# Where the 128-column scores stand among TensorE's attention products in a decoder layer

## The chip, the cores and the metric

The kernel runs on one core of a Trainium2 chip. The metric is the device time of one execution in microseconds (us). TensorE multiplies matrices, VectorE (DVE), ScalarE (ACT) and GpSimd (POOL) do the elementwise work, and SyncE (SP) issues most of the transfers.

## The reference

One layer over 1024 tokens of width 1024, in float32. The input is normalised and modulated, and one projection makes all that follows: a gated convolution branch of 31 taps, 24 attention heads of 64 columns in three groups of 8, and gates.

```python
# (window, dilation) of a group; a query attends keys t, t-d, ..., t-window
DILATION_GROUPS = ((128, 1), (512, 4), (2048, 16))
scores = jnp.einsum('bdhnqe,bdhnke->bdhnqk', qb, kb) * (e ** -0.5)
scores = jnp.where(mask, scores, NEG_INF)
m = jnp.max(scores, axis=-1)
p = jnp.exp(scores - m[..., None])
o = jnp.einsum('bdhnqk,bdhnke->bdhnqe', p, vb) / p.sum(-1)[..., None]
...
merged = sigmoid(g_conv) * y_conv + sigmoid(g_att) * y_att
x = rmsnorm(x + gate * (merged @ w_o)) * final_g
```

Within a group the sequence is cut into subsequences by the dilation, and a block of 128 queries sees its own block of keys and, where there is one, the block before it. The first group has a previous block for 7 of its 8 blocks of queries, the second for every other block, the third for none.

## The kernel before

**Precision.** A product of two float32 matrices is made of three products of parts: each operand is split into a high part and a low part, and high x high, high x low and low x high are added up in PSUM (`mm3`, lines 73 to 75, for the projections). For a score the parts of keys lie one under the other on the 128 partitions (64 rows high, 64 low), with the queries' high part twice, so that two products do: the keys with `q` (line 880), and with `ql`, the low part of the queries over zeros (line 881).

**Stages.** The start makes the normalised input; then follow the projections of the convolution branch, while DVE works through the taps; then the attention with the projections of keys, queries and one gate beside it; then the merge, the last product and the norm. TensorE, DVE, ACT and SP run in the order in which the code is written in the attention (a manual schedule).

**The attention** is a loop over slots (lines 1093 to 1140). A slot issues half of a half unit of projection (4 of 8 steps of 128 rows, 12 products of 512 columns, by `next(stream)`), and then the attention's own products of three stages that are in flight:

- `values` of the slot 4 earlier (line 916): the stationary operand is a block of values, 64 columns, the moving one the weights of the softmax in two parts, `ph` and `pl`. A product moves 256 columns of queries or 128. The code calls the first block's three products of 256 `wide`, the others `narrow`. The third group has only products of 128, all `narrow`.
- `turn` of the slot 2 earlier (line 895): transposes of 128 x 128 of the exponentials `sb`, 2 to 4 in a slot, with the unit matrix `ident`. ACT and DVE then split the transposed result into `ph` and `pl` (lines 713 and 716).
- `scores` of the slot itself (lines 880 and 881): the stationary operand is a block of queries, 128 columns; the moving one is a block of keys, 128 columns, or two blocks, 256. A slot takes two blocks of queries of one head, so it has four score products: two of 128 and two of 256, four of 256, or in the third group four of 128. DVE then adds the mask and finds the row's extreme (line 884), ACT takes the exponential (line 888).

A head pair `n` takes 8 slots, four for each head; `st_` counts them. The tile `s` of PSUM for scores has two buffers, and so has `sb`. Keys and queries reach the tiles `k2`, `q2` and `ql` of a head by SP's copies (line 812) from the parts that a projection left, slots ahead of the head's first score.

**The order within a slot** is written out by hand. Lines 1118 and 1119 lay the values and transposes in one row: transpose, wide value, transpose, the narrow values, wide value, transpose, wide value, transpose. That row is issued; then the scores are issued behind it, block by block of queries, high part and low part; then comes the next slot's projection.

Of the kernel before, what the change touches and what calls it, by code (L numbers as in the profile page):

```python
# [16 lines left out]
P = 128  # L17
# [22 lines left out]
def layer(ctx: ExitStack, tc: tile.TileContext, a, out):  # L40
    nc = tc.nc
# [131 lines left out]
    with sbuf_pool("start") as st, tc.manual_schedule(  # L173
# [168 lines left out]
        for kt in range(KT):  # L342
# [9 lines left out]
            c = slice(kt * P, (kt + 1) * P)  # L352
# [273 lines left out]
    for d in range(KT):  # L626
        w, sg_ = ahead
# [186 lines left out]
    def move_kq(n, part, h):  # L814
        i = turn_of(n, h)
        if not part:
            k2[n, h], q2[n, h] = head_tile(f"k{i}", "k2"), head_tile(f"q{i}", "q2")
        move(k2[n, h], 0, n, part, 0, 0, h)
        move(k2[n, h], 64, n, part, 0, 1, h)
        move(q2[n, h], 0, n, part, 1, 0, h)  # L820
        move(q2[n, h], 64, n, part, 1, 0, h)
        move(q_low[i], 0, n, part, 1, 1, h)
# [28 lines left out]
    class Attend:  # L851
# [19 lines left out]
        def scores(self, st_):  # L871
            tp, h, spans, o = self.spans(st_)
            stats = self.stats
            k, q, ql = k2[self.n, h], q2[self.n, h], self.ql[h]
            ps = psa.tile([P, 512], F32, name="s", tag="s")
            sb = self.sb[st_] = ap_.tile([P, 512], F32, name="sb", tag="sb", bufs=2)
            for t, c, w in spans:
                k0 = t * P + P - w
                ts_, ks = slice(t * P, (t + 1) * P), slice(k0, k0 + w)
                nc.tensor.matmul(ps[:, c:c + w], q[:, ts_], k[:, ks], start=True, stop=False)  # L880
                nc.tensor.matmul(ps[:, c:c + w], ql[:, ts_], k[:, ks], start=False, stop=True)  # L881
            for t, c, w in spans:
                mk = mask2 if self.g == 2 else mask[:, 256 - w:256]
                nc.vector.tensor_tensor_reduce(  # L884
                    out=sb[:, c:c + w], in0=ps[:, c:c + w], in1=mk, scale=-SCALE, scalar=3e38, op0=add, op1=ALU.min,
                    accum_out=stats[:, t, h, 1:2])
            for t, c, w in spans:
                nc.scalar.activation(sb[:, c:c + w], sb[:, c:c + w], AF.Exp, bias=stats[:, t, h, 1:2],  # L888
                                     scale=-1.0, accum_out=stats[:, t, h, 0:1])
# [182 lines left out]
    beside, heads, ahead_ao = {}, {}, []  # L1072

    def in_steps(it, slots):
        for x in slots:
            beside.setdefault(x, []).append(it)

    def moves(n, part, h):
        move_kq(n, part, h)
        yield  # L1080
# [11 lines left out]
    with tc.manual_schedule(engines={nc.tensor.engine, nc.vector.engine, nc.scalar.engine, nc.sync.engine}):  # L1092
        for slot_ in range(-LEAD, 4 * units - LEAD):
            due, lows[:] = lows[:], []
            for low in due:
                low()
            after, prepared = next(stream)

            wide, narrow, turns, rest = [], [], [], []
            if VAL <= slot_ < stages + VAL:  # L1100
                n, st_ = divmod(slot_ - VAL, 8)
                rest.append(heads[n].values(st_))
                wide, narrow = next(rest[0])
                if st_ == 7:
                    del heads[n]
            if TURN <= slot_ < stages + TURN:
                n, st_ = divmod(slot_ - TURN, 8)
                rest.append(heads[n].turn(st_))
                turns = [next(rest[-1]) for _ in range(0, heads[n].spans(st_)[3], P)]
            row = turns[:1] + wide[:1] + turns[1:2] * bool(wide) + narrow + wide[1:2]  # L1110
            row += turns[1 + bool(wide):3] + wide[2:] + turns[3:]
            assert len(row) == len(turns) + len(wide) + len(narrow)
            for product in row:
                product()
            for x in rest:
                assert next(x, None) is None
            if 0 <= slot_ < stages:
                n, st_ = divmod(slot_, 8)
                if st_ == 0:
                    heads[n] = Attend(n)  # L1120
                heads[n].scores(st_)
            for n, part in made:
                move_kq(n, part, 0)
                in_steps(moves(n, part, 1), [slot_ if n == 0 else slot_ + 1 if part else 8 * n - 4])
            made[:] = []
            if after:
                after()
            for c in beside.pop(slot_, ()):
                next(c)
            if prepared and prepared[1] < units:  # L1130
                prepared[0](prepared[1])
            if 0 <= slot_ < stages and st_ == 7:
                heads[n].store_stats()
                if order[n][1] == 2:
                    in_steps(combine(order[n][0]), [slot_ + 1 + x for x in STEPS])
        assert not beside and next(stream, None) is None
        for low in lows:
            low()
# [152 lines left out]
```

## Time and profile before

| | us |
|---|---|
| median of 3 runs | 1257.31 |
| lowest and highest | 1256.59 and 1257.95 |
| the profiled execution | 1258.8 |
| its span in the trace | 1257.0 |
| first score to last value, from the span's start | 672 to 1070 |

The profile is one execution recorded on the chip. Times are counted from the span's start. PE is TensorE's matmuls, PEld its loads of weights (the stationary operand), which overlap the matmuls; PEclk is the clock that TensorE was granted, in tenths of full speed. In a row of the timeline stand the start, the duration, the engine, the line of the code, the operation, the tiles (written<-read), then the stationary operand's shape (128*64 is 128 partitions by 64 columns) and the moving one's (128x256). In a row of groups, xN is the number of instructions, and behind the bar stand the busy time in us and the mean duration in ns. Matmuls are pipelined: their records overlap and their ends are modelled, so the distance between starts tells more than a duration.

### The profile page before, as it was taken

The page shows a single profiled execution, that of the slowest core. Times are in us where ns is not written, and L with a number is a line of the kernel's source. Part 1 is how long each engine was busy: PE and PEld are TensorE (multiplying, and loading weights), DVE is VectorE, ACT ScalarE, POOL GpSimd, SP SyncE. Part 2 cuts the span into 40 slices and gives each one's busy share as a digit, 9 for nine tenths or more (in the row PEclk, how much of TensorE's full clock was granted, in tenths as well). Part 3 has the DMA queues.
Part 4 walks back from the last instruction along what each step waited for, and adds up shares of the span by engine and source line. Part 5 has one row for each costly group of instructions (what it writes and reads, how often), then busy time and mean ns, then how long its engine had stood idle before and what let it go on. Part 6 is the DMA issues. An engine that isn't in the chain of part 4 may idle for free.

```text
span 1257.0 us, 16947 instructions
## 1 busy us (share of the span) xinstructions
PE 1233.3 (98%) x6208; PEld 1033.5 (82%) x6208; DVE 909.0 (72%) x1496; ACT 511.7 (41%) x1023; POOL 91.5 (7%) x79
## 2 busy tenths in 40 slices
PE   5999999999999999999999999999999999999997
PEld 4877888888888888888888888888888888887886
DVE  6776999999999986873325657777776762448554
ACT  4554202111222135931015656666666665345211
POOL 0000000000000000000031111111111012100000
PEclk9999999999999999999999999999999999999999
DMA  9531311311211112455636555665575563668231
GB/s 362 174 122 59 118 51 59 109 59 51 74 61 51 51 53 82 127 174 193 191 85 150 133 131 145 164 172 144 158 186 146 133 185 120 205 224 294 100 101 67
DMA packets 89751, 165.35 MB, mean 132 GB/s; under 512 B 28547, under 2 KB 42179, under 8 KB 89669
## 3 DMA queue, kind: packets, MB, share of 16 engines
q1 hardware_dynamic: 72992, 157.67, 42.0%
q10 hardware_dynamic: 16676, 6.61, 1.9%
q8 instruction: 49, 0.80, 0.3%
q14 instruction: 34, 0.27, 0.1%
HBM read 105.74 MB, written 27.04 MB: 106 GB/s over the span
## 4 chain that ended last, share of the span: by engine, by line
PE 94%; DMA 2%; DVE 1%; ACT 1%; issue 0%; SPq 0%; ACTq 0%; DVEq 0%
PE d L73 22%; PE d L75 22%; PE d L74 22%; PE o L916 4%; PE t L895 2%; PE d L1195 2%; PE d L1194 2%; PE d L469 2%; PE d L1196 2%; PE d L467 2%; PE d L468 2%; PE s L881 2%; PE s L880 2%; PE d L251 1%; PE d L249 1%; PE d L250 1%
## 5 line engine op out<-in xcount | busy, mean ns | idle before, releaser
L73 PE MATMUL d<-hh,whi 128*128 128x512 f32 x1072 | 421.4, 393 | 0.0
L74 PE MATMUL d<-hl,whi 128*128 128x512 f32 x1072 | 418.4, 390 | 1.9 <-DVE hl L349 1.9
L75 PE MATMUL d<-hh,wlo 128*128 128x512 f32 x1072 | 418.7, 391 | 0.0
L408 DVE SCALAR_TENSOR_TENSOR v<-u,cw,v 128x1024 f32<-128x1024 f32 x232 | 280.6, 1285 | 0.0
L75 PEld LDWEIGHTS d<-hh,wlo 128*128 128x128 f32 x1072 | 201.4, 188 | 42.6
L74 PEld LDWEIGHTS d<-hl,whi 128*128 128x128 f32 x1072 | 201.6, 188 | 41.4 <-DVE hl L349 2.8
L73 PEld LDWEIGHTS d<-hh,whi 128*128 128x128 f32 x1072 | 201.6, 188 | 38.9 <-issue 0.2
L57 ACT ACTIVATE whi<-wraw 128x512 fp32r<-128x512 f32 (+1 forms) x106 | 85.8, 830 | 212.7 <-PE d L74 204.8
L58 POOL TENSOR_TENSOR wlo<-wraw,whi 128x512 fp32r<-128x512 f32 (+1 forms) x56 | 82.1, 1481 | 644.0 <-ACT whi L57 643.9
L884 DVE CUSTOM_DVE_ANT_0 sb<-s,mask 128x128 f32<-128x128 f32 (+1 forms) x192 | 59.9, 350 | 68.3 <-PE s L881 67.7
L888 ACT ACTIVATE sb<-sb,stats 128x128 f32<-128x128 f32 (+1 forms) x192 | 84.9, 444 | 39.0 <-DVE stats L884 38.7
L916 PE MATMUL o<-ph,vt 128*64 128x128 f32 (+1 forms) x432 | 70.9, 270 | 0.0
L895 PE MATMUL t<-ident,sb 128*128 128x128 f32 x280 | 70.8, 274 | 0.0
L58 DVE TENSOR_TENSOR wlo<-wraw,whi 128x1024 fp32r<-128x1024 f32 (+1 forms) x50 | 57.4, 1149 | 14.7 <-ACT whi L57 14.1
L713 ACT ACTIVATE ph<-t 128x384 fp32r<-128x384 f32 (+2 forms) x96 | 45.7, 476 | 37.8 <-PE t L895 31.5
L916 PEld LDWEIGHTS o<-ph,vt 128*64 128x64 f32 x432 | 50.0, 135 | 8.8
L716 DVE TENSOR_TENSOR pl<-t,ph 128x384 fp32r<-128x384 f32 (+2 forms) x96 | 52.0, 542 | 4.2 <-ACT ph L713 3.7
L916 PE MATMUL o<-pl,vt 128*64 128x128 f32 (+1 forms) x216 | 52.9, 261 | 0.0
L1194 PE MATMUL d<-oh,hh 128*128 128x512 f32 (+1 forms) x136 | 51.3, 377 | 0.0
L1196 PE MATMUL d<-oh,hl 128*128 128x512 f32 (+1 forms) x136 | 51.3, 377 | 0.0
L880 PE MATMUL s<-k,q 128*128 128x128 f32 (+1 forms) x192 | 51.1, 291 | 0.0
L634 DVE TENSOR_TENSOR gs<-d,sgc 128x512 f32<-128x512 f32 x16 | 11.1, 692 | 54.9 <-PE d L75 48.9
(227 smaller groups left out, 1909.6 us busy)
## 6 DMA issues: line engine op xcount, KB each, us to landing
wraw<-in_w_t SPq DMA_DIRECT2D x67, 512.0 KB, 3.9
k<-kqp SPq DMA_DIRECT2D x96, 128.0 KB, 2.4
q<-kqp SPq DMA_DIRECT2D x96, 128.0 KB, 2.5
wa<-in_w_ada SPq DMA_DIRECT2D x16, 512.0 KB, 6.6
ql<-kqp SPq DMA_DIRECT2D x48, 128.0 KB, 2.4
wg<-wscr SPq DMA_DIRECT2D x48, 128.0 KB, 3.1
wraw<-in_w_v SPq DMA_DIRECT2D x11, 512.0 KB, 3.6
x<-in_xT SPq DMA_DIRECT2D x8, 512.0 KB, 10.2
```

The source lines that it names most:

```text
L57: nc.scalar.activation(hi, raw, AF.Copy)
L58: (lo_eng or nc.vector).tensor_sub(lo, raw, hi.bitcast(F32))
L73: nc.tensor.matmul(ps, lh, rh, start=start, stop=False)
L74: nc.tensor.matmul(ps, lh, rl, start=False, stop=False)
L75: nc.tensor.matmul(ps, ll, rh, start=False, stop=stop)
L408: nc.vector.scalar_tensor_tensor(d, u[:, k:k + S], cw[:, ct, k:k + 1], d, op0=mult, op1=add)
L880: nc.tensor.matmul(ps[:, c:c + w], q[:, ts_], k[:, ks], start=True, stop=False)
L888: nc.scalar.activation(sb[:, c:c + w], sb[:, c:c + w], AF.Exp, bias=stats[:, t, h, 1:2], scale=-1.0, accum_out=stats[:, t, h, 0:1])
L895: yield from ((lambda c=c: nc.tensor.transpose(ps[:, c:c + P], sb[:, c:c + P], ident)) for c in range(0, o, P))
L916: nc.tensor.matmul(out_, l, r, **kw))
L1194: nc.tensor.matmul(ps, hh[:, k, c], rh, start=k == 0, stop=False)
L1196: nc.tensor.matmul(ps, hl[:, k, c], rh, start=False, stop=k == KT - 1)
```

## The change

`scores` no longer issues its products itself. It hands them out as a list, with the width of each (128 or 256), and goes on to DVE's and ACT's part when it is called again. The loop over slots then builds the row of values and transposes as before, and marks each entry twice: whether it is light (a value, whose stationary operand has 64 columns) and whether it is long (a transpose or a value of 256 columns). Ahead of a light entry, where what stands before it is long (or nothing stands before it), it puts the next of the slot's short scores, those of 128 columns. Short scores that find no place are issued behind the row, and the scores of 256 columns behind those.

```diff
             for t, c, w in spans:
                 k0 = t * P + P - w
                 ts_, ks = slice(t * P, (t + 1) * P), slice(k0, k0 + w)
-                nc.tensor.matmul(ps[:, c:c + w], q[:, ts_], k[:, ks], start=True, stop=False)
-                nc.tensor.matmul(ps[:, c:c + w], ql[:, ts_], k[:, ks], start=False, stop=True)
+                for i, x in enumerate((q, ql)):
+                    products.append((w, lambda c=c, w=w, l=x[:, ts_], r=k[:, ks], i=i: nc.tensor.matmul(
+                        ps[:, c:c + w], l, r, start=i == 0, stop=i == 1)))
+            yield products
...
-            row = turns[:1] + wide[:1] + turns[1:2] * bool(wide) + narrow + wide[1:2]
-            row += turns[1 + bool(wide):3] + wide[2:] + turns[3:]
-            for product in row:
-                product()
...
+            short = [p for w, p in score if w == P]
+            row = []
+            for x, light, long_ in ([(x, False, True) for x in turns[:1]] + [(x, True, True) for x in wide[:1]] +
+                                    [(x, False, True) for x in turns[1:2] * bool(wide)] +
+                                    [(x, True, False) for x in narrow] + [(x, True, True) for x in wide[1:2]] +
+                                    [(x, False, True) for x in turns[1 + bool(wide):3]] +
+                                    [(x, True, True) for x in wide[2:]] + [(x, False, True) for x in turns[3:]]):
+                if short and light and (not row or row[-1][1]):
+                    row.append((short.pop(0), False))
+                row.append((x, long_))
+            for product, _ in row:
+                product()
+            for product in short + [p for w, p in score if w > P]:
+                product()
```

The order on the other engines stays: DVE, ACT, POOL and SP issue the same instructions in the same order. On TensorE the scores' line is 882 now, the transposes' 898 and the values' 919.

First, TensorE's queue in a slot of the second group, behind the projection's 12 products, before the change. `t<-ident,sb` is a transpose, `o<-ph,vt` and `o<-pl,vt` are values, `s<-k,q` and `s<-k,ql` scores; the numbers in 64x256 are the columns of weights and of the moving operand for values, and 128 partitions and moving columns for scores and transposes.

```order
L895 MATMUL t<-ident,sb 128x128
L916 MATMUL o<-ph,vt 64x256
L895 MATMUL t<-ident,sb 128x128
L916 MATMUL o<-ph,vt 64x128 x2
L916 MATMUL o<-pl,vt 64x128
L916 MATMUL o<-ph,vt 64x256
L895 MATMUL t<-ident,sb 128x128
L916 MATMUL o<-pl,vt 64x256
L880 MATMUL s<-k_4719,q_4720 128x128
L881 MATMUL s<-k_4719,ql 128x128
L880 MATMUL s<-k_4719,q_4720 128x256
L881 MATMUL s<-k_4719,ql 128x256
```

The same slot in TensorE's queue after the change:

```order
L898 MATMUL t<-ident,sb 128x128
L882 MATMUL s<-k_4719,q_4720 128x128
L919 MATMUL o<-ph,vt 64x256
L898 MATMUL t<-ident,sb 128x128
L882 MATMUL s<-k_4719,ql 128x128
L919 MATMUL o<-ph,vt 64x128 x2
L919 MATMUL o<-pl,vt 64x128
L919 MATMUL o<-ph,vt 64x256
L898 MATMUL t<-ident,sb 128x128
L919 MATMUL o<-pl,vt 64x256
L882 MATMUL s<-k_4719,q_4720 128x256
L882 MATMUL s<-k_4719,ql 128x256
```

The two short scores moved from the row's end to places behind the first and the second transpose, each ahead of a value; the two long scores now follow the last value.

Second, TensorE's queue in a slot whose values are of the third group and whose scores are as well, before the change:

```order
L895 MATMUL t<-ident,sb 128x128
L916 MATMUL o<-ph,vt 64x128 x2
L916 MATMUL o<-pl,vt 64x128
L916 MATMUL o<-ph,vt 64x128 x2
L916 MATMUL o<-pl,vt 64x128
L895 MATMUL t<-ident,sb 128x128
L880 MATMUL s<-k_5122,q_5123 128x128
L881 MATMUL s<-k_5122,ql 128x128
L880 MATMUL s<-k_5122,q_5123 128x128
L881 MATMUL s<-k_5122,ql 128x128
```

And after it:

```order
L898 MATMUL t<-ident,sb 128x128
L882 MATMUL s<-k_5122,q_5123 128x128
L919 MATMUL o<-ph,vt 64x128 x2
L919 MATMUL o<-pl,vt 64x128
L919 MATMUL o<-ph,vt 64x128 x2
L919 MATMUL o<-pl,vt 64x128
L898 MATMUL t<-ident,sb 128x128
L882 MATMUL s<-k_5122,ql 128x128
L882 MATMUL s<-k_5122,q_5123 128x128
L882 MATMUL s<-k_5122,ql 128x128
```

Here one short score of four moved, behind the first transpose; the other three stay behind the row.

More of the change, by code (lines that the diff above doesn't have):

```diff
@@ L874, in scores @@
             k, q, ql = k2[self.n, h], q2[self.n, h], self.ql[h]
+            products = []
             ps = psa.tile([P, 512], F32, name="s", tag="s")
@@ L1109, in layer @@
                 turns = [next(rest[-1]) for _ in range(0, heads[n].spans(st_)[3], P)]
-            row = turns[:1] + wide[:1] + turns[1:2] * bool(wide) + narrow + wide[1:2]
-            row += turns[1 + bool(wide):3] + wide[2:] + turns[3:]
-            assert len(row) == len(turns) + len(wide) + len(narrow)
-            for product in row:
-                product()
-            for x in rest:
-                assert next(x, None) is None
+            score = []
             if 0 <= slot_ < stages:
@@ L1120, in layer @@
                     heads[n] = Attend(n)
-                heads[n].scores(st_)
+                rest.append(heads[n].scores(st_))
+                score = next(rest[-1])
+            short = [p for w, p in score if w == P]
[8 more added lines that the diff above has]
+                row.append((x, long_))
+            assert len(row) - len([p for w, p in score if w == P]) + len(short) == len(turns) + len(wide) + len(narrow)
+            for product, _ in row:
+                product()
+            for product in short + [p for w, p in score if w > P]:
+                product()
+            for x in rest:
+                assert next(x, None) is None
             for n, part in made:
```

## The prediction

> **What bounds the kernel now.** I read the page first, for the busiest engine and its clock.
>
> ```profile
> span 1257.0 us, 16947 instructions
> PE 1233.3 (98%) x6208; PEld 1033.5 (82%) x6208; DVE 909.0 (72%) x1496; ACT 511.7 (41%) x1023; POOL 91.5 (7%) x79
> PEclk9999999999999999999999999999999999999999
> ```
>
> TensorE is busy for 98% of the span at full granted clock, so only its own steps can be shortened. Next the table of stretches for the attention, 672 to 1071 us (columns: stretch, its length, then busy time and instructions of PE, PEld, DVE, ACT and POOL, the clock, the share of the DMA engines), and the table of TensorE's waits over the whole program.
>
> ```profile
> 672.00:1071.00 399.00, 399.00 (x2507) 345.25 (x2507) 267.11 (x755) 246.50 (x679) 63.52 (x45) 1.00 0.58 151
> PE d L249 <- ACT wh L237: 12.5, 1, 12.5
> PE d L74 <- DVE hl L349: 1.9, 2, 1.1
> PE d L75 <- DVE wlo L58: 1.2, 1, 1.2
> PE d L251 <- DVE hl L230: 0.4, 1, 0.4
> ```
>
> In the attention TensorE never waits for anybody (none of the four waits is of an attention line), DVE works 267 of 399 us and ACT 247. What sets the time of this stage is how quickly one product follows the other. A matmul's own duration does not tell that, since products overlap in the records. The starts of the weight loads do: a load starts when the product before its own starts. So the time from the load of X to the next load is the step from the product before X to X. Here are the loads of one slot (start, duration; L895 transposes, L916 values, L880 and L881 scores, L73 to L75 the projection).
>
> ```profile
> 719.44 0.19 PEld L75 LDWEIGHTS d<-hh,wlo 128*128 128x128 f32 x1
> 719.67 0.14 PEld L895 LDWEIGHTS t<-ident,sb 128*128 128x128 f32 x1
> 719.90 0.13 PEld L916 LDWEIGHTS o<-ph,vt 128*64 128x64 f32 x1
> 720.01 0.14 PEld L895 LDWEIGHTS t<-ident,sb 128*128 128x128 f32 x1
> ...
> 720.29 0.14 PEld L916 LDWEIGHTS o<-pl,vt 128*64 128x64 f32 x1
> 720.35 0.14 PEld L916 LDWEIGHTS o<-ph,vt 128*64 128x64 f32 x1
> 720.43 0.14 PEld L895 LDWEIGHTS t<-ident,sb 128*128 128x128 f32 x1
> 720.53 0.14 PEld L916 LDWEIGHTS o<-pl,vt 128*64 128x64 f32 x1
> 720.64 0.19 PEld L880 LDWEIGHTS s<-k,q 128*128 128x128 f32 x1
> 720.76 0.19 PEld L881 LDWEIGHTS s<-k,ql 128*128 128x128 f32 x1
> 720.87 0.19 PEld L880 LDWEIGHTS s<-k,q 128*128 128x128 f32 x1
> 720.98 0.19 PEld L881 LDWEIGHTS s<-k,ql 128*128 128x128 f32 x1
> 721.10 0.19 PEld L73 LDWEIGHTS d<-hh,whi 128*128 128x128 f32 x1
> ```
>
> Each step is the longer of two things: the stream of the product before, and the load of this one. Behind a projection product of 512 columns it takes 0.23 (719.44 to 719.67), all stream. A value after a transpose takes 0.11 (719.90 to 720.01): the transpose is a long product. A value of 64 weight columns after a value of 128 columns takes 0.06 (720.29 to 720.35). A score, 128 weight columns, takes 0.11 after a score of 128 columns (720.76 to 720.87). Is that its load, or the stream of the score before it? The matmul records answer: there, the next record starts when the stream before it is over.
>
> ```profile
> 720.76 0.22 PE L880 MATMUL s<-k,q 128*128 128x128 f32 x1
> 720.82 0.27 PE L881 MATMUL s<-k,ql 128*128 128x128 f32 x1
> 720.93 0.33 PE L880 MATMUL s<-k,q 128*128 128x256 f32 x1
> ```
>
> The first short score really starts at 720.76 (the next load's start), and the second's record begins 0.06 later; the second really starts at 720.87 (the load of the third), and the third's record begins at 720.93, again 0.06 later. So a short score streams for 0.06 and the array then stands 0.05 until 128 columns of weights are in. Short scores in a row, and the long product behind them, pay 0.11 each for a stream of 0.06. That is the waste the change can touch.
>
> **The change, part by part.** Another slot, with four short scores in a row; the load at 753.16 is the fourth behind the one at 752.72.
>
> ```profile
> 752.29 0.13 PEld L916 LDWEIGHTS o<-pl,vt 128*64 128x64 f32 x1
> 752.35 0.20 PEld L916 LDWEIGHTS o<-ph,vt 128*64 128x64 f32 x2
> 752.47 0.13 PEld L916 LDWEIGHTS o<-pl,vt 128*64 128x64 f32 x1
> ...
> 752.72 0.19 PEld L881 LDWEIGHTS s<-k,ql 128*128 128x128 f32 x1
> ...
> 753.16 0.19 PEld L74 LDWEIGHTS d<-hl,whi 128*128 128x128 f32 x1
> ```
>
> *What a moved short score takes away.* One step at the end of the row. Three steps take 0.34 in the first slot (720.76 to 721.10), four take 0.44 here (752.72 to 753.16): 0.78 / 7 = 0.111 us.
>
> *What it costs in its new place*, behind a transpose or a long value and ahead of a value. Two steps stand where one stood. The step into the score: its load of 0.11 lies beside the transpose's stream, which the value had to sit out anyway. The next rows have that pair, transpose then score, 0.11 (686.53 to 686.64), the same as transpose then value above; I allow 0.002.
>
> ```profile
> 686.42 0.14 PEld L895 LDWEIGHTS t<-ident,sb 128*128 128x128 f32 x1
> 686.53 0.19 PEld L880 LDWEIGHTS s<-k,q 128*128 128x128 f32 x1
> 686.64 0.19 PEld L881 LDWEIGHTS s<-k,ql 128*128 128x128 f32 x1
> ```
>
> The step from the score to the value stands nowhere in this trace. It is the longer of the score's stream, 0.06 (the matmul records), and the load of 64 columns, 0.06: by the rows 720.29 to 720.35 and 752.29 to 752.47 (three steps, 0.18) that is four steps in 0.24. I take 0.060, since both parts are shown one by one. Below it I go no further than 0.056, as rounding of those rows allows. Above, the far end is 0.111, what every product behind a short score pays today; a middle row is 0.08, value to transpose (720.35 to 720.43), a pair of two kinds. That row gives its 0.02 back in the next step (0.10 instead of the 0.12 of 720.64 to 720.76), so I stay near 0.06.
>
> Per moved score: 0.111 - 0.002 - 0.060 = 0.049 us.
>
> *How many.* The score products of the program:
>
> ```profile
> L880 PE MATMUL s<-k,q 128*128 128x128 f32 x104 | 25.8, 264 | 0.0
> L881 PE MATMUL s<-k,ql 128*128 128x128 f32 x104 | 26.9, 275 | 0.0
> ```
>
> 208 are short. Counted through the changed order, slot by slot, 139 find a place: two in each of 36 slots (72), three in each of 16 (48), one in each of 19 (19). The other 69 stay at the row's end: a slot whose values are of the third group has six short values in a row behind one transpose, so only one place, and it is given four short scores. 139 x 0.049 = 6.8 us. In 24 of the slots with two a long score now follows a long value directly; that step is the 0.12 that a short score pays there today (720.64 to 720.76), and I take off 0.004 each as the rows' rounding allows: 0.1. The gain is **6.7 us**; the far ends are 139 x (0.109 - 0.111), 0.3 us lost, and 139 x (0.109 - 0.056), 7.4 won.
>
> *What comes free or late.* DVE's and ACT's work on a score is issued behind the same neighbours as before and no instruction is added, on the queues of SP and POOL neither. DVE can't be what is late next: it has 399 - 267 = 132 us of idle time in this stage against 6.7. TensorE's end of the stage moves by the whole gain, and the loads, stores and norms after it move with it.
>
> Against its own span the profiled run would be 1257.0 - 6.7 = 1250.3. That run took 1258.8 with what lies around the span, 1.5 over the median 1257.31, so I work from the median: 1257.3 - 6.7 = **1250.6 us**.
>
> A rule of the Trainium skill speaks against this change. "TensorE: Matmul & The Clock Gate", Part 3, "The mechanism", lists from other traces that a weight load overlaps a running matmul only where the two use different row groups (the paragraph before it allows a background buffer as well). All these products use 128 rows, so by it nothing is ever hidden; what follows from that is the second rival.
>
> **The rivals.** (1) *The middle price.* Score to value costs 0.08 because two kinds of product meet. Then 139 x (0.109 - 0.080) = 4.0, time 1253.3. For it: the value to transpose row. Against: its 0.02 came back at once. 5%.
>
> (2) *A product costs the same wherever it stands*: the load of a value behind a score is not hidden, or the value waits until all 128 columns are free, and pays 0.111. Nothing is won: 1257.6 by the far end above, 1257.3 if all prices are fixed. Against it: today's load of 0.19 for L75 begins at 719.44, when the product before it starts, and the step is still 0.23, the stream alone. The skill's rule would have load and stream add up there; the trace disagrees with it. For it: no score to value pair was ever seen. 5%, of which the skill's rule has one.
>
> (3) *Slower: the first score of a head comes too early for its keys and queries.* Of the 24 heads 23 have their first score, a short one, moved (the first head's slot has no transpose to go behind); it now stands behind the row's first transpose, 0.74 us earlier in the quoted slot (from 720.64 to 719.90) and, where the row has a fourth transpose ahead of the scores (0.11, 686.42 to 686.53), up to 0.85. TensorE works in order, so the values and transposes behind it would stand as well. As the scores wait for nothing today, no wait can exceed the move: at most 23 x 0.85 = 19.6, less the gain, 12.9 slower, 1270.2. It decides from 6.7 / 23 = 0.29 us per head on. The closest of them, by the last copy issued ahead of a head's first score, is here (SP's issues, the slowest landings of q and ql, then the load now behind the first transpose).
>
> ```profile
> 1020.89 1.22 SPq L812 DMA_DIRECT2D q<-kqp  x2
> 1022.16 0.59 SPq L812 DMA_DIRECT2D ql<-kqp  x1
> DMA to landing us min/median/max: 2.2/2.5/6.4
> DMA to landing us min/median/max: 2.2/2.4/6.0
> 1028.80 0.14 PEld L916 LDWEIGHTS o<-ph,vt 128*64 128x64 f32 x1
> ```
>
> With the slowest landing of the stage the last copy is there by 1022.16 + 6.0 = 1028.2, before the new start at 1028.8; with the median by 1024.6. 2%.
>
> **How the numbers follow.** Forecast 88%, rival (1) 5%, (2) 5%, (3) 2%. The forecast's own range is a price of 0.056 to 0.070 for score to value, 7.4 to 5.4 won, 1249.9 to 1251.9, and 0.7 on the lower side for the spread of the runs shown (1256.59 to 1257.95): 1249.2. Above it reaches to rival (1), 1253.3. What is left out is (2) and (3), 7%, and some 5% of the forecast's tails. A measurement of this kernel can tell 0.2%, 2.5 us, from no change. Faster by that: forecast and (1), 93%. Same: (2), 5%. Slower: (3), 2%.
>
> **What would show it.** Right: in the profile after, the load of a value behind a short score and the next load lie 0.06 apart; transpose to score is 0.11; the long scores at the row's end lie 0.12 apart as now; rows like the first are 0.10 us shorter, like the second 0.05; TensorE still has no wait in the attention; the span is near 1250.3. Wrong: 0.08 or 0.11 behind the moved scores (rivals 1 and 2), or scores that wait for copies at a head's first slot (rival 3). A change of time outside the attention would mean that I looked in the wrong place.

## The result, and the profile after

The changed kernel takes 1249.72 us (median of 4 runs, 1249.16 to 1250.70), beside it the kernel before 1257.63 (4 runs, 1256.59 to 1258.06): 7.9 us less by the medians, ratio 0.994, 95% interval 0.9929 to 0.9952.

The page after, first rows:

```profile
span 1248.2 us, 16947 instructions
PE 1226.6 (98%) x6208; PEld 1025.8 (82%) x6208; DVE 908.0 (73%) x1496; ACT 511.2 (41%) x1023; POOL 91.1 (7%) x79
```

As many instructions as before, and TensorE is still busy for 98% of the span; so the products stand closer together. Here are the loads of the first quoted slot after the change (start, duration; L882 scores, L898 transposes, L919 values).

```profile
718.01 0.14 PEld L898 LDWEIGHTS t<-ident,sb 128*128 128x128 f32 x1
718.24 0.19 PEld L882 LDWEIGHTS s<-k,q 128*128 128x128 f32 x1
718.35 0.14 PEld L919 LDWEIGHTS o<-ph,vt 128*64 128x64 f32 x1
718.43 0.14 PEld L898 LDWEIGHTS t<-ident,sb 128*128 128x128 f32 x1
718.53 0.19 PEld L882 LDWEIGHTS s<-k,ql 128*128 128x128 f32 x1
718.64 0.20 PEld L919 LDWEIGHTS o<-ph,vt 128*64 128x64 f32 x2
718.76 0.14 PEld L919 LDWEIGHTS o<-pl,vt 128*64 128x64 f32 x1
...
719.23 0.19 PEld L882 LDWEIGHTS s<-k,ql 128*128 128x128 f32 x1
719.35 0.19 PEld L73 LDWEIGHTS d<-hh,whi 128*128 128x128 f32 x1
719.47 0.19 PEld L74 LDWEIGHTS d<-hl,whi 128*128 128x128 f32 x1
```

The steps are read as in the prediction. Transpose to score takes 0.11 (718.24 to 718.35, and 718.53 to 718.64), as transpose to value did. From 718.64 to 718.76 lie two steps, score to value and value to value: 0.06 each. The first score to value step does not read so: from 718.35 to 718.43 it is 0.08, and the step from that long value to the transpose is 0.10 (718.43 to 718.53); the part on the prediction below comes back to this pair. The long scores at the end cost 0.12, as before (719.23 to 719.35). From the first transpose's load to the load at L74 the row takes 1.46 us; before it took 1.55, from 719.67 to this load:

```profile
721.22 0.19 PEld L74 LDWEIGHTS d<-hl,whi 128*128 128x128 f32 x1
```

And the slot with four short scores, after the change:

```profile
749.38 0.14 PEld L898 LDWEIGHTS t<-ident,sb 128*128 128x128 f32 x1
749.61 0.19 PEld L882 LDWEIGHTS s<-k,q 128*128 128x128 f32 x1
749.73 0.20 PEld L919 LDWEIGHTS o<-ph,vt 128*64 128x64 f32 x2
749.85 0.14 PEld L919 LDWEIGHTS o<-pl,vt 128*64 128x64 f32 x1
...
750.61 0.19 PEld L74 LDWEIGHTS d<-hl,whi 128*128 128x128 f32 x1
```

Two steps, score to value and value to value, in 0.12 again (749.73 to 749.85); the row takes 1.23 where it took 1.27, from this load of before to the one at 753.16:

```profile
751.89 0.14 PEld L895 LDWEIGHTS t<-ident,sb 128*128 128x128 f32 x1
```

The stretch from the load of the first score to that of the last value shows what the attention as a whole won. Before, then after:

```profile
671.83 0.19 PEld L880 LDWEIGHTS s<-k,q 128*128 128x128 f32 x1
1070.24 0.14 PEld L916 LDWEIGHTS o<-pl,vt 128*64 128x64 f32 x1
```

```profile
670.61 0.19 PEld L882 LDWEIGHTS s<-k,q 128*128 128x128 f32 x1
1062.69 0.14 PEld L919 LDWEIGHTS o<-pl,vt 128*64 128x64 f32 x1
```

398.41 us against 392.08: 6.3 less. The spans differ by 8.8, so 1.2 more went ahead of the attention (671.83 against 670.61) and 1.2 behind it (1257.0 - 1070.24 = 186.8 against 1248.2 - 1062.69 = 185.5), where both programs are the same. The waits of TensorE after:

```profile
PE d L249 <- ACT wh L237: 11.8, 1, 11.8
PE d L74 <- DVE hl L349: 1.7, 2, 1.1
PE d L251 <- DVE hl L230: 0.4, 1, 0.4
```

None is in the attention. The table of the loads has one short pause there, ahead of a transpose, for which it names no releaser:

```profile
PEld t L898 <- issue: 0.3, 1, 0.3
```

The wait of the merge (L75 for `wlo`, 1.2 us before) is gone, and the first wait of all is 0.7 shorter. Do these belong to the change? That is one thing to test.

### The profile page after: what moved, and what is told of

The parts are those of the page before. It is cut to its first block, busy times and chain, and to the rows that moved or that the text cites. A ratio compares the mean times of both kernels' runs of the same rounds, so it can differ in the third digit from the quotient of the medians.

```text
span 1248.2 us, 16947 instructions
## 1 busy us (share of the span) xinstructions
PE 1226.6 (98%) x6208; PEld 1025.8 (82%) x6208; DVE 908.0 (73%) x1496; ACT 511.2 (41%) x1023; POOL 91.1 (7%) x79
## 4 chain that ended last, share of the span: by engine, by line
PE 97%; DMA 1%; DVE 1%; ACT 1%; issue 0%; SPq 0%; ACTq 0%; DVEq 0%
PE d L73 23%; PE d L75 23%; PE d L74 23%; PE o L919 4%; PE s L882 3%; PE t L898 3%; PE d L1212 2%; PE d L1210 2%; PE d L469 2%; PE d L467 2%; PE d L1211 2%; PE d L468 2%; PE d L251 1%; PE d L249 1%; PE d L250 1%; DMA x<-in_xT 1%
## 5 line engine op out<-in xcount | busy, mean ns | idle before, releaser
L74 PE MATMUL d<-hl,whi 128*128 128x512 f32 x1072 | 418.1, 390 | 1.7 <-DVE hl L349 1.7
L75 PE MATMUL d<-hh,wlo 128*128 128x512 f32 x1072 | 418.4, 390 | 0.0
L75 PEld LDWEIGHTS d<-hh,wlo 128*128 128x128 f32 x1072 | 201.2, 188 | 42.9
L74 PEld LDWEIGHTS d<-hl,whi 128*128 128x128 f32 x1072 | 201.5, 188 | 41.4 <-DVE hl L349 2.6
L898 PE MATMUL t<-ident,sb 128*128 128x128 f32 x280 | 73.1, 274 | 0.0
L919 PE MATMUL o<-ph,vt 128*64 128x128 f32 (+1 forms) x432 | 68.1, 247 | 0.0
L882 PE MATMUL s<-k,q 128*128 128x128 f32 (+1 forms) x192 | 56.9, 302 | 0.0
L882 PE MATMUL s<-k,ql 128*128 128x128 f32 (+1 forms) x192 | 52.8, 285 | 0.0
L919 PE MATMUL o<-pl,vt 128*64 128x128 f32 (+1 forms) x216 | 52.6, 258 | 0.0
```

The lines of the kernel that those rows point to most:

```text
L74: nc.tensor.matmul(ps, lh, rl, start=False, stop=False)
L75: nc.tensor.matmul(ps, ll, rh, start=False, stop=stop)
L882: products.append((w, lambda c=c, w=w, l=x[:, ts_], r=k[:, ks], i=i: nc.tensor.matmul(ps[:, c:c + w], l, r, start=i == 0, stop=i == 1)))
L898: yield from ((lambda c=c: nc.tensor.transpose(ps[:, c:c + P], sb[:, c:c + P], ident)) for c in range(0, o, P))
L919: nc.tensor.matmul(out_, l, r, **kw))
```

## The experiments

The theory is the prediction's: the step to a product is the longer of the stream of the product before and the load of its own weights. A short score has a short stream and a long load, so it costs least where a long product stands ahead (its load is hidden) and a light one behind (the load there is as short as its stream). Both halves are needed. The rivals: it is enough that a light product follows; it is enough that a long one stands ahead; the gain comes from clearing the row's end; part of the gain comes from outside the attention.

**The kernel before once more**, without an edit.

> The kernel before once more, for its profile alone. In the first two profiles the stretch from the first score's load to the last value's is 398.4 us before and 392.1 after, 6.3 apart, and the spans are 8.8 apart: 1.2 us more lie ahead of the attention and 1.2 behind it, where the programs are the same. Theory (the gain is made of steps between products, in the attention alone): the stretch is 398.4 within 0.2 again, and what lies ahead of it and behind it moves by about 1 us from run to run. Rival (the change also helps the merge behind it): behind the attention there are 186.7 us again, within 0.2.

```profile
670.47 0.19 PEld L880 LDWEIGHTS s<-k,q 128*128 128x128 f32 x1
1069.39 0.14 PEld L916 LDWEIGHTS o<-pl,vt 128*64 128x64 f32 x1
```

This profile has a span of 1255.0. The stretch is 398.92, 0.5 more than the first time, where I had allowed 0.2. Behind it are 1255.0 - 1069.39 = 185.6 and not 186.8. Of TensorE's waits in it, two rows matter:

```profile
PE d L249 <- ACT wh L237: 11.4, 1, 11.4
...
PE t L895 <- DVE pl L716: 0.3, 1, 0.3
```

The merge's wait of 1.2 is absent here too, without the change; the start waits 11.4 instead of 12.5; and a transpose waits once for DVE, 0.3, which had not happened in the first profile. What lies ahead of and behind the attention differs by 1.4 and 1.2 us between two profiles of one kernel, so the rival on the merge falls.

**Only the first place of each slot.**

```diff
-            row = []
+            row, shorts = [], len(short)
...
-                if short and light and (not row or row[-1][1]):
+                if len(short) == shorts and short and light and (not row or row[-1][1]):
```

> Only the first place of each slot takes a short score: 71 of the 139 places. Theory (each moved score saves its own 0.045 to 0.049 us, whichever place it has): 3.2 to 3.5 us faster than before, the attention's stretch 394.9 to 395.2. Rival (the gain comes from the row's end, where no short score stands between the last value and the long scores any more): no place alone clears the row's end in the slots with two, so most of the gain is gone, under 1.5 us.

Measured: 1252.65 us against 1256.20, 3.6 less, ratio 0.9971 (0.9960 to 0.9982). The stretch:

```profile
670.68 0.19 PEld L882 LDWEIGHTS s<-k,q 128*128 128x128 f32 x1
1065.16 0.14 PEld L919 LDWEIGHTS o<-pl,vt 128*64 128x64 f32 x1
```

394.48, 3.9 less than the first profile before and 4.4 less than the second. The time agrees with the theory; the stretch won 0.4 to 1.2 more than the 3.2 to 3.5 of the sum and so missed the expected 394.9 to 395.2. The table of steps at the end of this section shows where that rest lies: the steps that the edit touches won 3.4. A place pays by itself; the rival of the cleared end allowed 1.5.

**As many scores, ahead of a value, but behind a short value.**

```diff
-                if short and light and (not row or row[-1][1]):
+                if places and short and light and i and entries[i - 1][1:] == (True, False):
                     row.append((short.pop(0), False))
+                    places -= 1
```

(`entries` is the list of the loop, `places` the number of places that the change finds in the slot.)

> As many short scores in the same slots, 139, each ahead of a value again, but behind a value of 128 columns and not behind a transpose or a long value. Theory (a step is the longer of the stream of the product before and the load of this one): the step into the score is now 0.111, the one out of it 0.060, against 0.060 for the value alone, so each moved score costs 0.111 and takes away 0.111: the time of before within 0.7 us, the stretch 398 to 399. Rival (it is enough that a light value follows): the gain of the change, 6 to 7 us.

Measured: 1256.33 against 1256.20, ratio 0.9999 (0.9990 to 1.0008). The whole gain is gone. The loads of the slot:

```profile
719.00 0.19 PEld L882 LDWEIGHTS s<-k,q 128*128 128x128 f32 x1
719.11 0.14 PEld L919 LDWEIGHTS o<-ph,vt 128*64 128x64 f32 x1
719.17 0.19 PEld L882 LDWEIGHTS s<-k,ql 128*128 128x128 f32 x1
719.28 0.14 PEld L919 LDWEIGHTS o<-pl,vt 128*64 128x64 f32 x1
```

Value to score is 0.11 (719.00 to 719.11, 719.17 to 719.28), score to value 0.06 (719.11 to 719.17). The light value behind is worth nothing when the score's own load isn't hidden. The stretch is 399.54, over the 399 that I had allowed; 0.8 of it is one wait for DVE, of the kind that the kernel before, run once more, showed with 0.3:

```profile
PE t L898 <- DVE pl L716: 0.8, 1, 0.8
```

```profile
670.52 0.19 PEld L882 LDWEIGHTS s<-k,q 128*128 128x128 f32 x1
1070.06 0.14 PEld L919 LDWEIGHTS o<-pl,vt 128*64 128x64 f32 x1
```

**As many scores, behind a projection product and ahead of another.** The slot's list of scores is made ahead of the projection's piece, and the piece takes them between its steps.

```diff
                     mm3(ps, hi[:, c], lo[:, c], hh[:, k, s], hl[:, k, s], k == 0, k == KT - 1)
+                    if between and k % 4 < 3:
+                        between.pop(0)()
...
+            between[:] = short[:places]
+            short = short[places:]
+            after, prepared = next(stream)
```

> As many short scores in the same slots, 139, each behind a projection product of 512 columns, but ahead of another one with 128 columns of weights, so no light value follows. Theory: the step into the score stays 0.227, all stream, and the step out of it is 0.111, the projection's load; each costs 0.111 and takes away 0.111: the time of before within 0.7 us, the stretch 398 to 399. Rival (a long product ahead is enough, as it hides the score's load): the gain of the change, 6 to 7 us. The first scores of a head come up to 3 us earlier than before here; should keys and queries then come too late, TensorE has waits at scores, which it had not.

Measured: 1257.70 against 1256.20, ratio 1.0011 (1.0002 to 1.0020): nothing won, slightly slower. The loads around two of the scores (here L886):

```profile
715.76 0.19 PEld L75 LDWEIGHTS d<-hh,wlo 128*128 128x128 f32 x1
716.00 0.19 PEld L886 LDWEIGHTS s<-k,q 128*128 128x128 f32 x1
716.23 0.19 PEld L73 LDWEIGHTS d<-hh,whi 128*128 128x128 f32 x1
716.34 0.19 PEld L74 LDWEIGHTS d<-hl,whi 128*128 128x128 f32 x1
```

The score's load is hidden (716.00 to 716.23, the stream of 512 columns), but the projection product behind it pays 0.11 for its own 128 columns (716.23 to 716.34) that its neighbour's stream used to hide. A long product ahead isn't enough either. The stretch is 400.24 (rows in the last section), over the 398 to 399 expected. TensorE has no wait in this attention, though the first scores of a head come far earlier than with the change: the copies of keys and queries are no bound.

**One score more, ahead of the row.** Where short scores remain, one goes behind the projection's last product and ahead of the first transpose, on top of the change.

```diff
...
+            places = sum(e[1] and (not i or entries[i - 1][2]) for i, e in enumerate(entries))
+            if len(short) > places and turns:
+                row.append((short.pop(0), False))
...
```

> The change, and in the 35 slots where short scores still stand behind the row one more of them goes ahead of the row's first transpose, behind the projection's last product. Its load is hidden by 512 columns; behind it comes a transpose, whose load the rows value to transpose put at 0.08 us, between a value's 0.06 and a score's 0.11. Theory (stream against load): each saves 0.111 - 0.080 = 0.03 us, 35 x 0.03 = 1.1 us beyond the change, the attention's stretch 391.0 against 392.1. Rival (a light value must follow, a transpose counts like 128 columns of weights): 0.0 beyond the change, the stretch 392.1. Rival (a transpose counts like a value): 35 x 0.05 = 1.8, the stretch 390.3.

Measured: 1248.77 against 1256.84 before, ratio 0.9934 (0.9920 to 0.9948); the change beside it, next below, 1249.81. The two ranges overlap, so the times alone don't tell them apart. The stretch does, and so do the loads of the slot with four short scores:

```profile
669.80 0.19 PEld L882 LDWEIGHTS s<-k,q 128*128 128x128 f32 x1
...
748.10 0.19 PEld L75 LDWEIGHTS d<-hh,wlo 128*128 128x128 f32 x1
748.33 0.19 PEld L882 LDWEIGHTS s<-k,q 128*128 128x128 f32 x1
748.55 0.14 PEld L898 LDWEIGHTS t<-ident,sb 128*128 128x128 f32 x1
748.61 0.19 PEld L882 LDWEIGHTS s<-k,ql 128*128 128x128 f32 x1
...
749.50 0.19 PEld L74 LDWEIGHTS d<-hl,whi 128*128 128x128 f32 x1
...
1059.64 0.14 PEld L919 LDWEIGHTS o<-pl,vt 128*64 128x64 f32 x1
```

Score to transpose takes 0.06 (748.55 to 748.61; 0.058 on average over the 35), not the 0.08 on which my number for the theory stood: the rival that a transpose counts like a value is right. From L75's load to L74's the slot takes 1.40; the change has 749.15 to 750.61, 1.46, by this row:

```profile
749.15 0.19 PEld L75 LDWEIGHTS d<-hh,wlo 128*128 128x128 f32 x1
```

The stretch is 389.84, 2.2 under the change's first profile and 2.0 under its second (below); the rival's sum was 35 x 0.05 = 1.8, and the table of steps below has 1.8. Why did I read 0.08? By the rule for reading the loads, 0.08 was never value to transpose. In the slot with six values after the change, 750.03 to 750.11 is the step into the last value, from a value, and 750.11 to 750.14 is the step from that value into the transpose: 0.08 and 0.03, two steps of 0.06 in sum. The transpose's load begins 0.02 late there, so the step before it reads longer and its own shorter.

```profile
750.03 0.13 PEld L919 LDWEIGHTS o<-pl,vt 128*64 128x64 f32 x1
750.11 0.14 PEld L898 LDWEIGHTS t<-ident,sb 128*128 128x128 f32 x1
750.14 0.22 PEld L882 LDWEIGHTS s<-k,ql 128*128 128x128 f32 x1
```

**The change once more**, without an edit.

> The change as it is, on the same chip and in the same rounds as the one above. Theory: the attention's stretch is 6.3 us shorter than before's 398.4 to 398.9, within 0.5, and of the 7.9 between the first medians what is over 6.3 was the runs' own spread ahead of the attention and behind it: over many runs the gain is 6.3 to 6.8, ratio 0.9946 to 0.9950. Rival (the change gains outside the attention too): 7.9 again, ratio 0.9937.

Measured: 1249.81 against 1256.84, 7.0 less, ratio 0.9941 (0.9928 to 0.9953). The stretch:

```profile
669.46 0.19 PEld L882 LDWEIGHTS s<-k,q 128*128 128x128 f32 x1
1061.33 0.14 PEld L919 LDWEIGHTS o<-pl,vt 128*64 128x64 f32 x1
```

391.87, against 398.92 of the second profile before: 7.05 less, where the first two differed by 6.33. The time lies between theory and rival, and its interval (0.9928 to 0.9953, 6 to 9 us) holds both; what speaks for the theory is the second profile before, whose parts ahead of and behind the attention were about as short as after the change.

**The stretches taken apart.** Each stretch is the sum of its steps between load starts. The table adds them up in two groups by the product that stands ahead: one of the attention (a transpose, value or score) or one of the projection. The moves within the row change the first group alone.

| profile | behind the attention's products, us | behind the projection's, us |
|---|---|---|
| before | 125.8 | 272.6 |
| before, once more | 125.8 | 273.1 |
| the change | 119.0 | 273.1 |
| the change, once more | 119.0 | 272.9 |
| only the first place | 122.4 | 272.1 |
| behind a short value | 125.9 | 273.7 |
| one score more, ahead of the row | 117.2 | 272.7 |

The first group repeats within 0.1 between two profiles of one kernel, and it says what the stretches blur: the change takes away 6.8 to 6.9 us, the first places alone 3.4, the places behind short values nothing, and the score ahead of the row another 1.8. The second group holds the pause ahead of one transpose: 0.5 in the second profile before (two steps take 0.96 in place of 0.46), which is all that its stretch was longer, 0.9 behind short values, and 0.1 in the first profile of the change. Without these pauses it is still 0.3 to 0.4 longer after the change than before, and 0.5 shorter with the first places alone. The moves within the row don't touch these steps, and the cause stays open.

## Why the prediction was right

**The bound.** Right: TensorE's steps set the time, and no other engine came in. TensorE's waits after the change have no row of the attention, and the one pause in its loads costs 0.1. The reason given for DVE, 132 us of idle time in the stage, was too coarse: in the second profile of the kernel before, one transpose did wait for DVE, at a cost of 0.5. The wait doesn't come from the change.

**The price that no row showed**, score to value, was taken at 0.060 from a stream of 0.06 and a load of 0.06. The profile after has 0.12 for that step and one known to be 0.06. At 87 of the 139 places the value's load and the next one lie 0.06 apart. At the other 52 they lie 0.083 apart, as from 718.35 to 718.43, and by the prediction's own sign this would be rival (1). There the value is a long one with a transpose behind it, and the step behind it is 0.100 (718.43 to 718.53) where behind a long value that itself follows a transpose it is 0.119. The two steps take 0.182 together, as against 0.181 at the 16 places where the long value is followed by a score. So the 0.02 isn't a cost of the moved score, and the prediction's sign should have been the sum of the two steps. Reading the matmul records for the stream, and the load starts for the real starts, was enough to price a pair of neighbours that had never stood together.

**The other terms.** Transpose to score was 0.11 as said. The number of places was right: the profile after has 139 steps from a short score to a value. The two quoted rows became 0.09 and 0.04 shorter, for 0.10 and 0.05 forecast. The 0.111 of a short score had a long score's step in it (720.98 to 721.10), without consequence: the 136 steps from short score to short score before the change take 0.111 on average. The sum of 6.7 compares with 6.8 to 6.9 for the steps that the moves change. That the two stretches give 6.33 and 7.05, 6.7 in the mean, is luck: one pair has a pause in the profile after, the other in the profile before, and both have the longer steps behind the projection's products.

**The size.** 7.9 by the first medians is 1.2 over the forecast, near the lower end of the range; the second measurement gives 7.0. In the first two profiles the surplus lies ahead of and behind the attention, in parts that the change doesn't touch and that differ as much between two profiles of the same kernel. That nothing is won there is not shown more closely than this.

**The rivals.** The middle price of 0.08 rested on the row 720.35 to 720.43, called value to transpose. By the prediction's own rule it is the step from a short value into a long one, and value to transpose is the next, 0.10 (720.43 to 720.53), behind a long stream; the row priced no pair of two kinds. It didn't enter the sum, but I used it a second time, in an expectation, and it failed. That a product costs the same wherever it stands is refuted by the pair of kernels with the scores behind short values and among the projection's: the same number of the same products in the same slots won 6 to 7 us or nothing, by their neighbours alone. The rule that the Trainium skill lists ("TensorE: Matmul & The Clock Gate", Part 3, "The mechanism": a load overlaps a running matmul only with different row groups) doesn't hold for these products of 128 rows: in the kernel with a score ahead of the row the score's load at 748.33, 0.19 long, lies inside a projection product's stream, a step of 0.22. The early first score met its keys and queries in time, even in the kernel that issues it within the projection.

## What to carry to other kernels

On an engine that is never idle, look at the steps between products and not at their durations: list them by pairs (what stands before, what this one must load), and the ones that are longer than the stream before them are, in these traces, waits for weights. Add a step that reads oddly to its neighbour before giving it a price. In this kernel a product with a short stream and 128 columns of weights belongs between one with a long stream and one with a light load; either neighbour alone brought nothing. About 0.05 us per product came from the order alone, with no instruction less.

## What the runs showed of the hardware

- A transpose has 128 columns in its stationary operand, yet the step into it behind a short stream is 0.06 us, as for 64 columns, where a score of 128 columns takes 0.11; its load record is 0.14 long, like a value's, and a score's 0.19. As the product ahead it counts as long: the step behind it is 0.11 for 128 moving columns, where a score's stream of as many is 0.06.
- A transpose's load begins 0.02 late behind a value that itself follows a short product (a value of 128 columns, or a score): the step before it then reads 0.08 in place of 0.06. Behind a value that follows a transpose it does not (the step before it is 0.109, as for values with no transpose behind). Behind a long value the next step gives the 0.02 back. Why it begins late stays open.
- Scores put between projection products, each writing another tile of PSUM, cost slightly more than the sum says: the stretch, by the rows below, is 400.24, 1.3 to 1.8 us over the two profiles before, about 0.01 for each of 139. Most of it lies in the steps from one projection product to the next, 0.233 in the pieces that hold such scores and 0.229 in the others. The cause wasn't tried.

```profile
670.06 0.19 PEld L886 LDWEIGHTS s<-k,q 128*128 128x128 f32 x1
1070.30 0.14 PEld L923 LDWEIGHTS o<-pl,vt 128*64 128x64 f32 x1
```
